# Hybrid attention and delta-rule layer on one core: solved blocks loaded ahead of the last head's copies, weight loads ordered behind casts, the last queries rotated on VectorE, the last results scaled on ScalarE

## The chip, the cores and the metric

The kernel runs on one core of one Trainium2 chip. The metric is device time in microseconds of one execution. The engines are TensorE (PE, with its weight loads as PEld), VectorE (DVE), ScalarE (ACT), GpSimd (POOL) and SyncE (SP). SP issues most DMAs, ACT issues the loads of the input weights; a queue issues its DMAs in the order in which they were placed on it.

## The reference

One layer for 1024 latent tokens and 256 context tokens of width 1024. Both are normalised and modulated (shift and scale from `c`), and go through one input projection of 4112 columns. Half of the mixing width is neighbourhood attention (8 heads of 64, a window of 8 x 16 in a 16 x 64 grid, plus all context keys in one softmax, with a learned bias). The other half is a gated delta rule in chunks, in both directions, with 4 heads of 128:

```python
a = jnp.where(pos[:, None] > pos[None, :],
              jnp.einsum('nbhid,nbhjd->nbhij', kb, k) * decay, 0.0)
t_inv = lax.linalg.triangular_solve(eye + a, ..., lower=True, unit_diagonal=True)
u = jnp.einsum('nbhij,nbhje->nbhie', t_inv, v * beta[..., None])
w = jnp.einsum('nbhij,nbhjd->nbhid', t_inv, kb * jnp.exp(gc)[..., None])
def step(state, xs):
    v_new = u_n - w_n @ state
    o_n = q_n @ state + qk_n @ v_new
    state = state * gl_n + k_n.T @ v_new
```

Its queries, keys and values go through a convolution over five tokens and SiLU; queries and keys are normalised, and those of the latent tokens are rotated by two axial angles. The scan's results are normalised. Both halves are multiplied by a SiLU gate each, concatenated, projected by `w_out`, normalised and added to the input.

## The kernel before, in words

Float32 products are made of three matmuls of split numbers: a weight is loaded raw, cast to its high part on ACT, and the low part is the difference, taken on POOL, or on DVE for every second quarter of the weights "nv0" (`load_w`, lines 550 to 573). The raw, high and low parts have 3, 4 and 4 buffers, which all input weights share.

The instructions are written in one order, and a planner that simulates the engines then puts the instructions of each engine in an order of its own: what is ready in its simulation goes by the order of writing, which `tc.high_priority(offset=n)` moves forward, and `order(r, before)` (line 169) keeps one instruction behind another without adding a wait. On the chip each engine works strictly in the order so planned.

The stages are these. `phase0` does the norms and the first projections. `phase2` (line 922) goes over the four heads of the delta rule. For each, it convolves Q, K and V (steps of one letter), turns Q and K to tokens and rotates them (T, `qk_tok`, line 1026), turns V (U), turns Q and K back (B), and, a head later, makes the chunk matrices (F, `delta_front`, line 1141). R is a part of the output gate. The letters p stand for one unit each of other projections (`projections`, line 981): three gates, then pair 1 of the attention, then the attention values in five units with the weights nv0, then pairs 2 and 3. 18 units come before the pairs 2 and 3, of which 14 stand in `phase2`'s strings of letters (lines 972) and 4 at the start of `phase_a2` (line 1644).

The inverse of each chunk's 128 x 128 matrix is made from 32 x 32 blocks. `delta_front` writes its matrices to `pm_dram`, and four DMAs copy their diagonal blocks to `ab_dram` (line 1175). There are 320 blocks in three groups. Two groups of 120 (heads 0 to 2) are solved together on DVE by `inv_pairs` (line 1195), in 30 levels of two operations, between the steps of head 3; the solved blocks are stored in `yd` (line 1216). The last 80 (head 3) are solved by `inv_blocks` (line 1218) in `phase_a2`. `inv_merge` (line 1241) then puts the blocks of a head together, in six parts named l, t, z, u, w, e in the string `MERGES` (line 138): l loads the matrices (pm, line 1247) and the solved blocks (vl, line 1258), t turns them with DVE's block transpose, z and u, w and e are small matmuls with copies between them, and e stores the result `tm`. One tm buffer serves the second direction of all four heads. `phase_a2` runs through the last 14 projection units with two generators beside them: `blocks` (the last group, then the masks and the loads of attention pair 0) and `merges`, at 4 and 1.5 steps per unit.

`phase_b` then interleaves the attention (`na_attn`, line 727) with the scan (`delta_scan`, line 1350), and `phase4` does the output projection. At the end of a pair's half, `values` in `na_attn` takes the reciprocal of twice the softmax sums (lines 762 and 763) and POOL spreads it over 512 elements (line 767); after a transposition on PE (line 773) it scales the result. `delta_end` (line 1457) scales a head's results by the norm's root; for the last head on DVE, in two halves (line 1471). `rsqrt` (line 196) adds and takes the power on POOL. "rho" is the root of the queries' norms of all heads; it is made in `delta_load` of head 0 (line 1345).

## Time and profile before

| | |
|---|---|
| median of 3 runs | 859.28 us (858.21 to 862.28) |
| profiled execution | 858.73 us, span 857.0 us |
| PE, PEld | 821.8 us (96%), 703.2 us (82%) |
| DVE, ACT, POOL | 498.9, 415.1, 359.1 us |
| granted PE clock, mean | 0.978 |

The profile is one execution, taken by the hardware profiler. Times in its rows count from the start of the span. A row of a window gives the stretch, its length, the busy time of PE, PEld, DVE, ACT and POOL with the number of instructions, the clock granted to PE as a share of full speed, the share of time in which the DMA engines were busy, and the GB/s they moved. A row of the order in time gives start, length, engine, line and operation, output and inputs, and in brackets the idle time before it with what ended it. A row of waits gives who waited for whom, the sum in us, the times, and the longest.

### The profile page before, as it was taken

The page shows a single profiled execution, that of the slowest core. Times are in us where ns is not written, and L with a number is a line of the kernel's source. Part 1 is how long each engine was busy: PE and PEld are TensorE (multiplying, and loading weights), DVE is VectorE, ACT ScalarE, POOL GpSimd, SP SyncE. Part 2 cuts the span into 40 slices and gives each one's busy share as a digit, 9 for nine tenths or more (in the row PEclk, how much of TensorE's full clock was granted, in tenths as well). Part 3 has the DMA queues.
Part 4 walks back from the last instruction along what each step waited for, and adds up shares of the span by engine and source line. Part 5 has one row for each costly group of instructions (what it writes and reads, how often), then busy time and mean ns, then how long its engine had stood idle before and what let it go on. Part 6 is the DMA issues. An engine that isn't in the chain of part 4 may idle for free.

```text
span 857.0 us, 16622 instructions
## 1 busy us (share of the span) xinstructions
PE 821.8 (96%) x6170; PEld 703.2 (82%) x6170; DVE 498.9 (58%) x998; ACT 415.1 (48%) x1089; POOL 359.1 (42%) x433
## 2 busy tenths in 40 slices
PE   8999999999999999979988999999999999999996
PEld 6788887888888778769876888888888988878885
DVE  4673454556376677699718953456556666653242
ACT  3372535654654753742215433566666666734121
POOL 0042221454482483562542202556747569525121
PEclk9999999999999999999997999799999999999998
DMA  8986442255526718723697599995958934134261
GB/s 333 337 293 214 142 129 89 86 173 185 144 86 212 225 51 275 196 80 116 212 237 234 177 256 273 412 247 192 279 154 271 238 114 160 39 111 135 98 197 50
DMA packets 86343, 159.67 MB, mean 186 GB/s; under 512 B 18405, under 2 KB 45750, under 8 KB 84086
## 3 DMA queue, kind: packets, MB, share of 16 engines
q1 hardware_dynamic: 78774, 144.94, 53.6%
q10 hardware_dynamic: 7488, 13.67, 5.5%
q8 instruction: 49, 0.80, 0.4%
q14 instruction: 32, 0.26, 0.1%
HBM read 109.51 MB, written 52.42 MB: 189 GB/s over the span
## 4 chain that ended last, share of the span: by engine, by line
PE 78%; DVE 8%; DMA 6%; ACT 3%; issue 3%; SPq 1%; POOL 1%; ACTq 0%; DVEq 0%; POOLq 0%
PE py L1525 3%; PE py L1527 3%; PE py L1526 3%; PE pz L587 3%; PE pz L588 3%; PE pz L583 3%; PE pa L1415 3%; PE pa L1426 2%; PE po L917 2%; PE tr L900 2%; PE po L912 2%; PE sc L882 2%; PE pv L598 2%; PE pv L597 2%; PE pv L596 2%
## 5 line engine op out<-in xcount | busy, mean ns | idle before, releaser
L887 ACT ACTIVATE pt<-pt,nm 128x544 f32<-128x544 f32 (+1 forms) x64 | 50.5, 790 | 39.2 <-DVE nm L886 38.8
L886 DVE CUSTOM_DVE_ANT_0 pt<-sc,gm 128x544 f32<-128x544 f32 (+1 forms) x64 | 49.4, 772 | 32.6 <-PE sc L882 27.0
L870 POOL TENSOR_TENSOR gm<-gt,mk 128x288 f32<-128x288 f32 (+1 forms) x48 | 46.5, 972 | 28.8 <-DVE nm L886 28.5
L1387 POOL TENSOR_SCALAR kd<-kt,kd 128x128 f32<-128x128 f32 x72 | 42.7, 605 | 25.2 <-PE pa L1426 20.7
L1015 DVE SCALAR_TENSOR_TENSOR acc_v<-xp_v,cols,acc_v 128x1282 f32<-128x1282 f32 x16 | 33.8, 2111 | 27.3 <-ACT acc_v L1013 26.9
L1168 POOL TENSOR_SCALAR_AFFINE_SELECT qe<-qe 128x256 f32<-128x256 f32 x32 | 28.9, 906 | 40.7 <-DVE qe L1167 40.7
L1591 DVE TENSOR_TENSOR finv<-py,ggb 128x512 f32<-128x512 f32 (+1 forms) x17 | 10.7, 657 | 50.7 <-ACT finv L1590 42.3
L583 PE MATMUL pz<-hh,wh_gz 128*128 128x512 f32 x96 | 39.1, 408 | 0.0
L587 PE MATMUL pz<-hl,wh_gz 128*128 128x512 f32 x96 | 39.1, 407 | 0.0
L588 PE MATMUL pz<-hh,wl_gz 128*128 128x512 f32 x96 | 39.0, 406 | 0.0
L1149 ACT ACTIVATE em<-em,gc 128x128 f32<-128x128 f32 x80 | 25.5, 390 | 25.2 <-DMA em<-gc_dram 23.9
L598 PE MATMUL pv<-wl_nv,hh 128*128 128x264 f32 x104 | 30.9, 300 | 4.8 <-DVE wl_nv L566 4.8
L1429 DVE SCALAR_TENSOR_TENSOR s<-s,egl,pa 128x128 f32<-128x128 f32 x64 | 19.7, 344 | 27.2 <-PE pa L1426 27.2
L1164 DVE SCALAR_TENSOR_TENSOR pm<-pk,nsc,em 128x128 f32<-128x128 f32 x80 | 23.5, 344 | 18.8 <-PE pk L1157 13.4
L1393 POOL TENSOR_SCALAR vb<-v,beta 128x128 f32<-128x128 f32 x40 | 24.1, 604 | 19.5 <-DVE y L1399 17.5
L900 PE MATMUL tr<-c,pt 128*96 128x128 f32 (+1 forms) x192 | 32.2, 277 | 0.0
L898 ACT COPY tcx<-tc 128x256 f32<-128x256 f32 x64 | 23.4, 366 | 16.1 <-PE tc L896 15.7
L566 POOL TENSOR_TENSOR wl_gz<-wr_gz,wh_gz 128x512 fp32r<-128x512 f32 x12 | 15.5, 1294 | 37.5 <-ACT wh_gz L565 35.9
L903 ACT COPY tl<-tr 96x384 f32<-96x384 f32 (+1 forms) x64 | 30.5, 476 | 0.0
L597 PE MATMUL pv<-wh_nv,hl 128*128 128x264 f32 x104 | 30.3, 294 | 0.0
L596 PE MATMUL pv<-wh_nv,hh 128*128 128x264 f32 x104 | 29.6, 296 | 0.0
L1415 PE MATMUL pa<-y,tm 128*128 128x128 f32 x144 | 25.3, 296 | 4.5 <-DVE y L1399 4.5
(470 smaller groups left out, 2853.1 us busy)
## 6 DMA issues: line engine op xcount, KB each, us to landing
wada<-in_w_ada SPq DMA_DIRECT2D x16, 512.0 KB
em<-gc_dram SPq DMA_DIRECT2D x20, 256.0 KB
pm_dram<-pm SPq DMA_DIRECT2D x20, 256.0 KB
tm_dram<-tm SPq DMA_DIRECT2D x8, 640.0 KB
kk<-qk_dram SPq DMA_DIRECT2D x16, 320.0 KB
tm<-tm_dram SPq DMA_DIRECT2D x4, 1280.0 KB
kq_dram<-kq SPq DMA_DIRECT2D x4, 1152.0 KB
kq<-kq_dram SPq DMA_DIRECT2D x4, 1152.0 KB
```

The lines of the kernel that those rows point to most:

```text
L583: r = nc.tensor.matmul(ps, wh, xh, start=(k == 0 and first), stop=False)
L587: nc.tensor.matmul(ps, wh, xl, start=False, stop=False)
L588: nc.tensor.matmul(ps, wl, xh, start=False, stop=(k == KC - 1))
L596: nc.tensor.matmul(ps, xh, wh, start=(k == 0), stop=False)
L597: nc.tensor.matmul(ps, xl, wh, start=False, stop=False)
L598: nc.tensor.matmul(ps, xh, wl, start=False, stop=(k == KC - 1))
L870: r = nc.gpsimd.tensor_tensor(self.gm[hh][:, 384 - n:384].rearrange("p (n c r) -> p n c r", c=nco, r=4), gv, self.mk[:, mo:mo + n].rearran ...
L886: nc.vector.tensor_tensor_reduce(pt[:, 384 - n:], sc[:, 512 - n:768], gm[:, 384 - n:], -1.0, 3.0e38, ALU.add, ALU.min, nm)
L887: self.last_exp = nc.scalar.activation(pt[:, 384 - n:], pt[:, 384 - n:], AF.Exp, bias=nm, scale=-1.0, accum_out=sums[:, ct, hh:hh + 1]).in ...
L900: self.pe(nc.tensor.transpose(pl[:m, rc * P:(rc + 1) * P], pt[:, 384 + (rc - 3) * m:384 + (rc - 2) * m], self.ident))
L1387: r = nc.gpsimd.tensor_scalar(kd[d], kt_[:, t, :], self.kd[:, h, d, t:t + 1], None, ALU.mult)
L1415: self.pe(nc.tensor.matmul(pa, tm[:, d, t, :], y[d], start=True, stop=True))
```

## The change

- **SP's queue.** The four copies of head 3's diagonal blocks leave `delta_front` and are issued in `blocks`, behind the loads of vl of the merge that has been issued by then. The loads of pm stand behind vl. The masks and pair 0's loads stand behind a vl, too.
- **ACT's queue.** A weight's load stands behind the cast before last.
- **DVE.** The additions of `inv_pairs` stand behind the last weight split written before them; a step has three levels in place of two. The rotation of the last head's queries moves from POOL to DVE.
- **POOL.** The root rho stands behind the last root taken before it. The spread of the reciprocals multiplies by 0.5, and the doubling on DVE is gone.
- **Order of writing.** The strings of `phase2` and `MERGES` change; nv0 is loaded one unit earlier; one more unit stands in `phase2` and one fewer at the start of `phase_a2`; the first step of `blocks` is moved forward by 800 in place of 300. With `while not self.vl_last: yield` that first step now returns without an instruction.
- **ACT** scales the last head's results, in eight operations.

```diff
-MERGES = "0l 0t 1l 0z 1t 0u 0w 2l 0e 1z 1u 2t 1w 1e 3l 2z 2u 3t 2w 2e 3z 3u 3w 3e"
+MERGES = "0l 0t 1l 0z 1t 0u 0w 0e 2l 1z 1u 2t 1w 3l 1e 2z 2u 2w 3t 2e 3z 3u 3w 3e"
...
-    def rsqrt(self, pool, x, n, tag, eps):
+    def rsqrt(self, pool, x, n, tag, eps, after=None):
         y = pool.tile([P, n], F32, name=f"rq_y_{tag}", tag=f"rq_y{n}")
-        self.nc.gpsimd.tensor_scalar(y, x, eps, None, ALU.add)
-        self.nc.gpsimd.tensor_tensor(y, y, bc(self.mhalf, [P, n]), ALU.pow)
+        r = self.nc.gpsimd.tensor_scalar(y, x, eps, None, ALU.add)
+        if after:
+            self.order(r, after)
+        self.last_root = self.nc.gpsimd.tensor_tensor(y, y, bc(self.mhalf, [P, n]), ALU.pow).ins.name
...
-            (load or nc.scalar.dma_start)(raw.rearrange("p k n -> p (k n)"), bass.AP(
+            r = (load or nc.scalar.dma_start)(raw.rearrange("p k n -> p (k n)"), bass.AP(
...
-                nc.scalar.copy(hi, raw)
-                (nc.vector if halves > 2 and k0 % 4 else nc.gpsimd).tensor_tensor(lo, raw, hi.bitcast(F32), ALU.subtract)
+                if r and len(self.casts) > 1:
+                    self.order(r, self.casts[-2])
+                self.casts.append(nc.scalar.copy(hi, raw).ins.name)
+                r = (nc.vector if halves > 2 and k0 % 4 else nc.gpsimd).tensor_tensor(lo, raw, hi.bitcast(F32), ALU.subtract)
+                self.split = r.ins.name
...
-            nc.vector.tensor_scalar(rs, sums[p, rt].rearrange("p a b -> p (a b)"), 2.0, None, ALU.mult)
-            nc.vector.reciprocal(rs, rs)
+            nc.vector.reciprocal(rs, sums[p, rt].rearrange("p a b -> p (a b)"))
...
-            nc.gpsimd.tensor_copy(rb[j], bc(rs.unsqueeze(2), [P, 8, 64]))
+            nc.gpsimd.tensor_scalar(rb[j], bc(rs.unsqueeze(2), [P, 8, 64]), 0.5, None, ALU.mult)
...
-                for c in ("RVpppTUpB", "RppVTpUBp", "RVTpUpB", "VRppTppUB")[h]:
+                for c in ("RpVppTUpB", "RppVpTpUB", "RVTpUpB", "VRppTpppUB")[h]:
...
-        yield from self.na_proj(pool, self.ps, [1])
-        w = self.load_w(self.wp, [(1024, 264)], 264, "nv0", halves=4)
+        for i, _ in enumerate(self.na_proj(pool, self.ps, [1])):
+            if i == 6:
+                w = self.load_w(self.wp, [(1024, 264)], 264, "nv0", halves=4)
+            yield
...
-                    eng = nc.gpsimd if which else nc.vector
+                    eng = nc.gpsimd if which and h < 3 else nc.vector
...
+        if h < 3:
+            self.inv_blocks_out(h)
+
+    def inv_blocks_out(self, h, after=None):
         ad, pd = self.ab_dram[:, :], self.pm_dram[h][:, :, :, :]
         for b in range(4):
-            nc.sync.dma_start(bass.AP(ad.tensor, ...
+            r = self.nc.sync.dma_start(
+                bass.AP(ad.tensor, ...
+            if after:
+                self.order(r, after)
...
-            nc.vector.tensor_tensor(ab[:, :, 0:m, m + 1:], ab[:, :, 0:m, m + 1:], t3, ALU.add)
-            if m % 2 == 0:
+            r = nc.vector.tensor_tensor(ab[:, :, 0:m, m + 1:], ab[:, :, 0:m, m + 1:], t3, ALU.add)
+            if self.split:
+                self.order(r, self.split)
+            if m % 3 == 0:
...
-            nc.sync.dma_start(pm[d][0:96], self.pm_dram[h][0:96, d])
...
-            nc.sync.dma_start(vl[32 * b:32 * b + 20], self.yd[g][10 * i:10 * i + 20].rearrange("t j i -> t (j i)"))
+            r = nc.sync.dma_start(vl[32 * b:32 * b + 20], self.yd[g][10 * i:10 * i + 20].rearrange("t j i -> t (j i)"))
+        self.vl_last = r.ins.name
+        for d in range(2):
+            self.order(nc.sync.dma_start(pm[d][0:96], self.pm_dram[h][0:96, d]), self.vl_last)
...
-            self.rho = self.rsqrt(self.cp, self.ssq.rearrange("p h t -> p (h t)"), 32, "rho", 4 * EPS)
+            self.rho = self.rsqrt(self.cp, self.ssq.rearrange("p h t -> p (h t)"), 32, "rho", 4 * EPS, self.last_root)
...
-                sl = slice(4 * gr, 4 * gr + 4)
-                nc.vector.tensor_tensor(o[:, sl], o[:, sl], bc(r[:, sl].unsqueeze(2), [P, 4, P]), ALU.mult)
+                for t in range(4 * gr, 4 * gr + 4):
+                    nc.scalar.activation(o[:, t, :], o[:, t, :], AF.Copy, scale=r[:, t:t + 1])
...
             def blocks():
+                while not self.vl_last:
+                    yield
+                self.inv_blocks_out(3, self.vl_last)
...
+                self.gate = self.vl_last
                 self.load(self.mk, self.I["masks"])
+                self.gate = None
...
+                self.gate = self.vl_last
                 self.na_pairs = {0: self.na_load(None, 0)}
+                self.gate = None
...
-            for _ in range(4):
+            for _ in range(3):
                 next(pr)
...
-                            with tc.high_priority(offset=300):
+                            with tc.high_priority(offset=800):
```

More of the change, by code (lines that the diff above doesn't have):

```diff
@@ L971, in phase2 @@
                     blocks = self.inv_pairs(cv)
-                for c in ("RVpppTUpB", "RppVTpUBp", "RVTpUpB", "VRppTppUB")[h]:
+                for c in ("RpVppTUpB", "RppVpTpUB", "RVTpUpB", "VRppTpppUB")[h]:
                     step(h, c)
-                    next(blocks, None)
+                    if h < 3 or c not in "":
+                        next(blocks, None)
             step(3, "F")
@@ L1172, in delta_front, with inv_load, inv_groups, inv_blocks_out @@
                 nc.sync.dma_start(self.qe_dram[h][:, :, t0 - 2:t0, :], qe)
+        if h < 3:
+            self.inv_blocks_out(h)
+    def inv_blocks_out(self, h, after=None):
         ad, pd = self.ab_dram[:, :], self.pm_dram[h][:, :, :, :]
         for b in range(4):
-            nc.sync.dma_start(bass.AP(ad.tensor, ad.offset + (80 * h + 20 * b) * 1024, [[32, 32], [1024, 20], [1, 32]]),
-                              bass.AP(pd.tensor, pd.offset + 32 * b * (20 * P + 1), [[20 * P, 32], [P, 20], [1, 32]]))
+            r = self.nc.sync.dma_start(
+                bass.AP(ad.tensor, ad.offset + (80 * h + 20 * b) * 1024, [[32, 32], [1024, 20], [1, 32]]),
+                bass.AP(pd.tensor, pd.offset + 32 * b * (20 * P + 1), [[20 * P, 32], [P, 20], [1, 32]]))
+            if after:
+                self.order(r, after)
+    def inv_load(self, g, ab):
+        nc = self.nc
+        n = min(120, 320 - 120 * g)
+        nc.sync.dma_start(ab[:n], self.ab_dram[120 * g:120 * g + n])
+        ab = ab[:n].rearrange("p (a b) -> p a b", a=32)
+        return ab
+    def inv_groups(self, gs, tile):
+        abs_ = [self.inv_load(g, tile(f"ab{g}", S)) for g in gs]
+        vbs = [tile(f"vb{g}", S) for g in gs]
+        tb = tile(f"tb{gs[0]}", 256 * len(gs))
+        yield
+        yield from self.inv_blocks(gs, abs_, vbs, [tb[:, 256 * i:256 * i + 256] for i in range(len(gs))])
+    def inv_blocks_out(self, h, after=None):
+        ad, pd = self.ab_dram[:, :], self.pm_dram[h][:, :, :, :]
+        for b in range(4):
+            r = self.nc.sync.dma_start(
+                bass.AP(ad.tensor, ad.offset + (80 * h + 20 * b) * 1024, [[32, 32], [1024, 20], [1, 32]]),
+                bass.AP(pd.tensor, pd.offset + 32 * b * (20 * P + 1), [[20 * P, 32], [P, 20], [1, 32]]))
+            if after:
+                self.order(r, after)
     def inv_load(self, g, ab):
@@ L1604, in phase_a2 @@
         with tc.tile_pool(name="a2", bufs=1, side="right", reuse_waits="tile") as ap:
-            ready = self.ready
+            ready, self.vl_last = self.ready, None
             buf = lambda nm, tag, n: self.pf.tile([P, n], F32, name=f"{nm}_{tag}", tag=tag)
             def blocks():
+                while not self.vl_last:
+                    yield
+                self.inv_blocks_out(3, self.vl_last)
                 vv = buf("ab", "vv", 2 * S)
@@ L1675, in run @@
             self.setup(ctx)
+            self.casts, self.split = [], None
             dt = lambda nm, shape: self.dp.tile(shape, F32, name=nm)
```

## The prediction

> **What bounds the kernel now.** I read the page first, then the waits of TensorE (PE), then the rows of the clock, then the chain of waits and the order in time around each stretch where PE stands still.
>
> ```profile
> span 857.0 us, 16622 instructions
> PE 821.8 (96%) x6170; PEld 703.2 (82%) x6170; DVE 498.9 (58%) x998; ACT 415.1 (48%) x1089; POOL 359.1 (42%) x433
> ...
> PE tz L1280 <- DVE ld L1268: 5.7, 1, 5.7
> PE pv L598 <- DVE wl_nv L566: 4.8, 1, 4.8
> ```
>
> PE is busy for 96% of the span, so a microsecond of the other engines is worth something only where PE waits for them, or where PE runs slowly. Two single waits make 10.5 us. The windows give what follows each (columns: stretch; length; PE, PEld, DVE, ACT and POOL busy; granted clock; DMA share; GB/s).
>
> ```profile
> 382.70:388.70 6.00, 6.00 (x28) 6.00 (x29) 5.73 (x11) 4.20 (x18) 6.00 (x4) 0.52 0.36 115
> 453.20:460.20 7.00, 6.99 (x91) 5.88 (x92) 5.32 (x8) 5.28 (x13) 3.06 (x5) 0.51 0.86 285
> 527.60:543.00 15.40, 13.54 (x221) 12.29 (x221) 7.03 (x16) 4.70 (x11) 8.41 (x16) 0.64 0.87 333
> 760.00:770.00 10.00, 8.19 (x53) 5.77 (x52) 6.89 (x9) 1.76 (x6) 5.04 (x5) 1.00 0.62 234
> ```
>
> After each long wait PE works at half the clock: 6.0 x 0.48 = 2.9 us and 7.0 x 0.49 = 3.4 us more. So the first hole (weights of nv0) costs 4.8 + 2.9 = 7.7 us, the second (solved blocks) 5.7 + 3.4 = 9.1 us. The third stretch, where the last merges have no projection beside them, costs 1.9 us idle and 15.4 x 0.36 = 5.5 us of clock. The last head's end costs 1.8 us idle, at full clock.
>
> **The first hole.** PE waits for a split of nv0 (line 566) that VectorE (DVE) does late:
>
> ```profile
> 378.64 2.98 POOL L1061 TENSOR_TENSOR tok<-tok,rot 128x512 f32<-128x512 f32 x2
> 379.05 1.45 DVE L1208 TENSOR_TENSOR tb<-ab 120x336 f32<-120x336 f32 x1
> 380.53 1.45 DVE L1210 TENSOR_TENSOR ab<-ab,tb 120x336 f32<-120x336 f32 x1
> 381.91 0.74 DVE L566 TENSOR_TENSOR wl_nv<-wr_nv,wh_nv 128x528 fp32r<-128x528 f32 x1
> 389.30 0.65 DVE L1208 TENSOR_TENSOR tb<-ab 120x468 f32<-120x468 f32 x1
> 381.58 5.71 POOL L199 TENSOR_TENSOR rq_y_rho<-rq_y_rho,mhalf 128x32 f32<-128x32 f32 x1
> 387.27 0.25 POOL L198 TENSOR_SCALAR rq_y_g<-ss 128x10 f32<-128x10 f32 x1
> ...
> L1059 DVE TENSOR_TENSOR rot<-tok,rope x8: 681/685/689, 181.8 to 396.0; 128x512 f32<-128x512 f32 x8
> ```
>
> While POOL rotates the last head's queries, a block step of 336 elements takes DVE 1.45 us; later, with POOL in its power function, one of 468 takes 0.65. The change takes these six POOL operations (6 x 1.49, half of 2.98, is 8.9 us) and gives DVE six of 0.69 = 4.1 us; four block operations of the rows shown or like them fall by about 0.9 each, so DVE comes out about even here. What helps PE is the order: nv0 (four loads, casts and splits) is issued one step earlier, and the later block additions stand behind its last split. A block operation already ahead of it, and the rotation's 4.1 us, can still delay it. I take 6.5 of the 7.7 us as gained; bounds 0 (the rotation and the block levels issued before it, now three to a step in place of two, stand ahead of it instead) and 7.7. The rho root (0.52 + 5.71 us on POOL) moves behind the key root: keys come up to 5.7 us earlier, and rho is next wanted only by the scan's ends, far later.
>
> **The second hole.** SyncE's queue and then the chain of waits show it:
>
> ```profile
> 429.07 2.60 SPq L1175 DMA_DIRECT2D ab_dram<-pm_dram  x4
> 431.76 1.03 SPq L1216 DMA_DIRECT2D yd<-ab  x2
> 436.59 1.17 SPq L1184 DMA_DIRECT2D ab_vv<-ab_dram  x1
> 437.81 1.21 SPq L1247 DMA_DIRECT2D pmf<-pm_dram  x2
> 439.41 2.05 SPq L1258 DMA_DIRECT2D vl<-yd  x4
> ...
> 440.84 8.78 DMA vl<-yd
> 453.21 2.34 PE tz L1280 x80
> ```
>
> The solved blocks (yd) are stored only after four copies of the last head's blocks have been issued, and loaded (vl) only after the last group's load and two loads of pm; they land 8.8 us after that, among the copies' small packets. The change moves those copies (four DMAs, 2.6 us of issue) and the group load behind vl, and the two pm loads too; the masks and pair 0's loads are held behind a vl as well. So yd can go at least 431.76 - 429.07 = 2.7 us earlier in the queue and vl another 2.4 (the rows of 436.59 and 437.81), and it lands without the copies beside it: the last head's vl, which has none, is waited for 4.99 us (row of 506.07 below), 3.8 less than 8.8. That is 8.9 us, before the earlier keys, against 5.7 needed. What is late next is pm, which the same matmuls read. I take 7.5 of 9.1 us; bounds 0 and 9.1.
>
> The clock is where a rule bears on this. The Trainium skill, TensorE: Matmul & The Clock Gate, Part 1, says that a gate halves PE's clock after about 3.4 us without work and gives it back after about as long a busy stretch. The rows above agree with the halving after 4.8 and 5.7 us, though the slow stretches last 6 to 7 us. By that rule a wait that is only cut below 3.4 us loses its whole slow stretch, too; by the rows alone, in proportion, half a wait would leave half of 2.9 and 3.4 us. It would raise case C below by 1.7 us of gain and leave the forecast.
>
> **What is late next: the last head's own merge.** Its blocks are inverted last, on DVE, and no projection covers the end:
>
> ```profile
> 496.26 0.19 DVE L1233 TENSOR_TENSOR ab_vv<-ab_vv,tb_qh 80x31 f32<-80x31 f32 x1
> 506.07 1.25 DVE L1266 STREAM_TRANSPOSE vx<-vl 128x1024 f32<-128x1024 f32 x1 [4.99 <-DMA vl<-yd]
> 529.85 1.96 POOL L1289 COPY tm<-ld 32x320 f32<-32x320 f32 x4 [18.04 <-DMA tm_dram<-tm]
> 527.53 0.24 PE pz L588
> 536.97 0.72 PE sc L879 x2
> 430.00:440.00 10.00, 10.00 (x55) 8.59 (x54) 0.69 (x1) 1.50 (x3) 8.03 (x9) 1.00 0.94 285
> 462.00:497.00 35.00, 35.00 (x552) 28.38 (x551) 32.31 (x73) 14.74 (x31) 7.10 (x8) 1.00 0.57 180
> ```
>
> From 442 (its load issued at 436.59) to 496.4 the group's solve shares a DVE that is busy 32.3 of 35 us. The copies now start after vl, so its load stays near 437 even if vl moves up by some 8 us; and the first call of its generator, which carries the raised priority (800), now only returns, since vl is not yet issued. PE arrives 14 us earlier (6.5 + 7.5). The chain gains about 6 us from merge work that DVE does earlier (it was busy 0.69 of the 10 us from 430), 3 of the 9.8 us between 496.3 and 506.1, as pair 0's loads now stand behind vl, and about 2 from the new merge order, which has head 2's "w" before head 3's "t" and so stores the shared tm sooner. 14 - 11 = 3 us come back: +3. Bounds: -7.4 (third stretch gone) and +9 (the chain gains only 5).
>
> **The rest.**
>
> ```profile
> 310.00:320.00 10.00, 8.44 (x46) 6.67 (x46) 4.80 (x6) 4.40 (x15) 8.85 (x10) 1.00 0.09 27
> 763.17 3.44 DVE L1471 TENSOR_TENSOR o<-o,rq_y_o 128x512 f32<-128x512 f32 x2 [2.40 <-POOL rq_y_o L1464]
> 767.36 0.63 PE L773 MATMUL prt<-c,rb 128*128 128x128 f32 x4 [1.63 <-DVE zs L760]
> L1418 ACT ACTIVATE vn<-pa,beta x40: 347/366/381, 543.2 to 756.3; 128x128 f32<-128x128 f32 x40
> L762 DVE TENSOR_SCALAR rs<-sums x8: 160/182/2067, 561.5 to 753.0; 128x8 f32<-128x8 f32 x8
> L767 POOL COPY rb<-rs x8: 599/612/618, 565.5 to 753.6; 128x512 f32<-128x512 f32 x8
> 593.17 0.60 POOL L767 COPY rb<-rs 128x512 f32<-128x512 f32 x1
> 598.09 0.60 PE L773 MATMUL prt<-c,rb 128*128 128x128 f32 x4
> L1387 POOL TENSOR_SCALAR kd<-kt,kd x72: 592/603/629, 540.0 to 745.8; 128x128 f32<-128x128 f32 x72
> ```
>
> Scaling on ScalarE: eight operations by 0.37 = 2.9 us in place of 3.44 on DVE, on an engine busy 1.76 of 10 us there. DVE's product of line 760 no longer stands behind them, and PE's wait of 1.63 goes: -1.7; bounds 0 and -1.8. The eight doublings of line 762 go: 8 x 0.18 and one of 2.07, at most -2. In their place the POOL copy of 0.61 us becomes a multiplication over 512 elements: from 0.61 (the copy) to 4 x 0.605 = 2.4 (line 1387 scaled up), that is 0 to +1.8 each, 0 to 14.5 us of POOL in all, for a result that PE wants some 4 us after it is there in the pair of rows shown (593.8 against 598.1). Where that cover is gone the whole could come to PE. I take 0 for the pair, bounds -2 and +6. The GPSIMD Engine Reference of the Trainium skill, section 4.1, calls one-input work there about line rate, which would make it 0.6; no row here shows a multiplication of this size, and by it the sum stays as it is.
>
> Before 370 us, where steps move one place: PE idles there once, 1.6 us in the row from 310. Loads on ScalarE's queue now stand behind the cast before last: their issue (0.33 us) adds no semaphore, it only keeps two weight halves in flight in place of three, while PE needs 24 matmuls of 0.23 us, 5.5 us, for two. I take 0; bounds -1.6 and +3 (one missed half).
>
> Sum against the profiled execution's 858.73 us (span 857.0 and 1.7 around it): -6.5 - 7.5 + 3 - 1.7 = -12.7, 846.0. The median shown, 859.28, lies 0.55 higher: 846.5.
>
> **Rivals.** A is the forecast.
> B, nothing comes back at the end: both holes whole, the third stretch half gone: -7.7 - 9.1 - 3.7 - 1.8 = -22.3, 837. For it: DVE's idle time from 430; against: the shared tm.
> C, only the first hole goes, and PE waits for pm or for vl's buffers in place of vl: -6.5 - 1.7 + 1 = -7.2, 852. For it: pm now follows vl, and vl's memory is cleared at line 1254 only when the front's last tiles are free.
> D, it does not do what it says: DVE, busy 19.45 of 20 us from 370 to 390, gets the rotation ahead of the split, the wait only changes its name, and the end takes back the rest: 0 - 7.5 + 9 - 1.7 = -0.2, 859.
>
> ```profile
> 370.00:390.00 20.00, 14.32 (x88) 13.43 (x87) 19.45 (x24) 10.66 (x46) 19.23 (x12) 0.83 0.23 71
> ```
>
> E, slower: the last head's copies start too late. If vl is issued no earlier than now, they go at 441.5 in place of 429.07, 12.4 us later; the solve, head 3's merge and the first scores follow by as much, and all that PE saved is waited for there: 858.73 + 12.4 - 1.7 - 3 = 866.4, 867 in the median's terms. It decides from about 9 us of delay of the copies on; against it stand the earlier yd and the 9.8 us of slack between 496.3 and 506.1.
>
> **How the numbers follow.** Chances: A 0.50 (own range 841 to 852), B 0.13, C 0.14, D 0.12, E 0.11. Half a per cent, 4.3 us, is about what a measurement of this kernel tells from no change. Faster: A, B and most of C, 0.75; within: D and a little of C, 0.14; slower: E, 0.11. The range leaves out E and about half of B: 836 to 861.
>
> **What would show it.** Right: no wait of line 598 for line 566 near 380 and a clock row of 1.00 there; vl issued before pm and before the copies, landing in under 5 us; no wait over 2 us of line 1280; on PE, line 773 without its 1.63. The last stretch before the scores should be longer than 9.4 us (527.5 to 537.0). Wrong: a clock row near 0.5 between 370 and 470, the last group's solve ending after 500, or line 773 waiting for line 767.

## The result, and the profile after

The changed kernel takes 863.76 us (median of 16 runs, 859.85 to 866.35), the kernel before 858.37 us beside it (16 runs, 853.34 to 862.87). The ratio is 1.0059, with a 95% interval of 1.0039 to 1.0080: slower by 0.6%, where 846.5 us was forecast. Its profiled execution takes 865.87 us, with a span of 864.2 us against 857.0.

Executions of one kernel differ by some ten microseconds, and a profile shows only one of them. So the stages below are compared as distances inside one profile, and the verdicts rest on the ratios.

First the stages on PE (windows; columns as in the prediction), for the kernel before and for the changed one:

```profile
370.00:400.00 30.00, 24.32 (x170) 23.43 (x169) 29.31 (x40) 12.57 (x51) 19.68 (x12) 0.89 0.27 83
400.00:440.00 40.00, 40.00 (x245) 35.86 (x244) 24.45 (x60) 9.10 (x18) 18.98 (x22) 1.00 0.66 212
440.00:470.00 30.00, 24.31 (x294) 19.49 (x293) 20.40 (x39) 12.09 (x25) 7.11 (x8) 0.83 0.88 240
...
527.00:560.00 33.00, 30.78 (x368) 27.41 (x368) 15.24 (x40) 15.11 (x41) 18.80 (x30) 0.79 0.93 360
```

```profile
370.00:400.00 30.00, 27.76 (x216) 26.66 (x215) 25.29 (x49) 15.82 (x56) 14.45 (x6) 1.00 0.34 106
400.00:440.00 40.00, 37.45 (x211) 32.35 (x211) 30.69 (x65) 8.51 (x17) 20.03 (x22) 1.00 0.63 201
440.00:470.00 30.00, 24.79 (x302) 19.96 (x301) 15.84 (x24) 12.97 (x27) 6.79 (x9) 0.89 0.89 222
...
527.00:560.00 33.00, 20.04 (x199) 18.42 (x200) 7.68 (x19) 8.04 (x21) 12.66 (x21) 0.59 1.04 373
```

The first hole is nearly gone: 27.76 of 30 us at full clock, where PE had 24.32 at 0.89. But 2.5 us are missing from 400 to 440, where none were, the second hole has hardly shrunk, and from 527 to 560 PE is busy for 20 us at a clock of 0.59, where it had 30.8 at 0.79. The waits of PE in the changed kernel, from 370 to 560, name what stands there:

```profile
PE tz L1357 <- POOL tm L1333: 10.9, 1, 10.9
PE tu L1343 <- issue: 3.2, 1, 3.2
PE tu L1343 <- ACT zt L1328: 3.2, 2, 3.0
PE pk L588 <- DVE sl_q L664: 2.1, 1, 2.1
PE tz L1324 <- DVE ld L1312: 2.0, 1, 2.0
PE pv L603 <- POOL wl_nv L570: 1.5, 1, 1.5
```

(Lines of the changed kernel are some 40 higher behind 1200: L1324 is L1280 of the kernel before, L1333 is L1289, L1357 is L1313, L1370 is L1326.) Line 588 waits for an operation that DVE does right behind the end of the pairs' solve. The wait of 10.9 us is head 3's "w", which needs POOL's copy into the shared tm, which needs the stores of head 2's tm. In order of time, SP, DVE, POOL and PE of the changed kernel:

```profile
431.63 0.22 DVE L1250 TENSOR_TENSOR ab<-ab,tb 120x60 f32<-120x60 f32 x1
...
431.88 0.79 SPq L1258 DMA_DIRECT2D yd<-ab  x2
437.35 1.41 SPq L1299 DMA_DIRECT2D vl<-yd  x4
...
447.66 3.61 SPq L1299 DMA_DIRECT2D vl<-yd  x4
453.93 3.58 SPq L1212 DMA_DIRECT2D ab_dram<-pm_dram  x4
...
461.37 0.39 SPq L1224 DMA_DIRECT2D ab_vv<-ab_dram  x1
...
503.02 0.19 DVE L1275 TENSOR_TENSOR ab_vv<-ab_vv,tb_qh 80x31 f32<-80x31 f32 x1
...
522.80 0.39 PE L593 MATMUL pz<-hh,wl_gz 128*128 128x512 f32 x1
...
531.56 0.33 SPq L1370 DMA_DIRECT2D tm_dram<-tm  x1
534.74 1.05 SPq L1370 DMA_DIRECT2D tm_dram<-tm  x1
...
542.23 1.96 POOL L1333 COPY tm<-ld 32x320 f32<-32x320 f32 x4 [33.48 <-DMA tm_dram<-tm]
...
548.29 0.58 PE L883 MATMUL sc<-kk,qh 128*128 128x256 f32 x1
...
808.26 0.60 ACT L1634 ACTIVATE finv<-py 128x512 f32<-128x512 f32 x1 [9.50 <-PE py L1571]
```

and the answering rows of the kernel before:

```profile
426.03 0.22 DVE L1210 TENSOR_TENSOR ab<-ab,tb 120x60 f32<-120x60 f32 x1
...
527.36 0.39 PE L588 MATMUL pz<-hh,wl_gz 128*128 128x512 f32 x1
...
536.90 0.58 PE L879 MATMUL sc<-kk,qh 128*128 128x256 f32 x1
...
801.13 0.60 ACT L1590 ACTIVATE finv<-py 128x512 f32<-128x512 f32 x1 [9.80 <-PE py L1527]
```

In this profile the pairs' solve ends 5.6 us later; not all of that is the kernel's (see "The first hole" below). The last head's copies leave at 453.93 and not at 429.07: behind head 2's load of solved blocks, not head 0's. The last group's solve ends 6.8 us later (503.02 against 496.26). From there to the first scores it is 45.3 us where it was 40.6 (536.90 less 496.26): 4.6 more. From the first scores to the first row of the last output it is 260.0 where it was 264.2: 4.2 less. 6.8 + 4.6 - 4.2 is the 7.2 us of the span. That PE ends the projections 4.6 us earlier (522.80 against 527.36) is in none of these terms: it is waited out. These are the terms of two profiles, not of the kernels.

### The profile page after: what moved, and what is told of

Its sections match the earlier page's. It is cut to its first block, busy times and chain, and to the rows that moved or that the text cites. A ratio compares the mean times of both kernels' runs of the same rounds, so it can differ in the third digit from the quotient of the medians.

```text
span 864.2 us, 16623 instructions
## 1 busy us (share of the span) xinstructions
PE 819.9 (95%) x6170; PEld 699.3 (81%) x6170; DVE 490.8 (57%) x994; ACT 419.5 (49%) x1097; POOL 359.4 (42%) x427
## 4 chain that ended last, share of the span: by engine, by line
PE 69%; DVE 11%; DMA 10%; ACT 3%; POOL 3%; issue 2%; SPq 1%; ACTq 0%; DVEq 0%; POOLq 0%
PE py L1569 4%; PE py L1571 3%; PE py L1570 3%; PE pz L588 3%; PE pz L593 3%; PE pz L592 3%; PE pa L1459 3%; DMA kk<-qk_dram 2%; PE po L921 2%; PE pa L1470 2%; PE tr L904 2%; PE po L916 2%; PE sc L886 2%; DMA pm_dram<-pm 2%; PE gpl_k L588 2%
## 5 line engine op out<-in xcount | busy, mean ns | idle before, releaser
L1022 DVE SCALAR_TENSOR_TENSOR acc_v<-xp_v,cols,acc_v 128x1282 f32<-128x1282 f32 x16 | 30.7, 1919 | 30.4 <-ACT acc_v L1020 17.8
L1333 POOL COPY tm<-ld 32x320 f32<-32x320 f32 x16 | 7.2, 452 | 61.1 <-DMA tm_dram<-tm 54.4
```

The lines of the kernel that those rows point to most:

```text
L1022: nc.vector.scalar_tensor_tensor(av, xp[:, s0 + tap:s0 + tap + 1282 - s0], wc(tap), av, ALU.mult, ALU.add)
```

## The experiments

The theories are C (the copies leave late and all behind them follows), S (the store's place in SP's queue), G (the gate on pair 0's loads), D (the DMA engines), T (what PE wins before the scores is waited out there), and those of the single parts. Every kernel is held against the kernel before on the same chip, and the changed kernel's ratio to it is 1.0059. e1 to e4 ran on one chip, e5 to e8 on a second, e9 to e15 on a third. The distances in the text are read from these rows of each profile (the starts of the first copy, of the solve's last operation and of the first scores):

| run | ratio (95%) | copies of head 3 | last solve ends | first scores | distance |
|---|---|---|---|---|---|
| before | 1 | 429.07 | 496.26 | 536.90 | 40.6 |
| changed | 1.0059 (1.0039 to 1.0080) | 453.93 | 503.02 | 548.29 | 45.3 |
| e1 | 1.0054 (1.0030 to 1.0078) | 446.94 | 496.38 | 540.77 | 44.4 |
| e2 | 1.0035 (1.0012 to 1.0058) | 436.03 | 495.28 | 545.26 | 50.0 |
| e3 | 1.0006 (0.9986 to 1.0026) | 418.90 | 495.47 | 543.17 | 47.7 |
| e4 | 1.0062 (1.0039 to 1.0084) | 449.94 | 503.55 | 543.35 | 39.8 |
| e5 | 1.0011 (0.9983 to 1.0039) | 419.22 | 496.09 | 543.21 | 47.1 |
| e6 | 0.9949 (0.9923 to 0.9975) | 418.41 | 497.13 | 538.58 | 41.5 |
| e7 | 0.9928 (0.9896 to 0.9960) | 427.78 | 494.78 | 535.45 | 40.7 |
| e8 | 1.0014 (0.9983 to 1.0045) | 425.00 | 494.78 | 536.13 | 41.4 |
| e9 | 0.9962 (0.9935 to 0.9990) | 415.20 | 490.19 | 530.77 | 40.6 |
| e10 | 0.9970 (0.9942 to 0.9999) | 429.52 | 497.42 | 538.10 | 40.7 |
| e11 | 0.9974 (0.9948 to 1.0000) | 426.94 | 493.72 | 531.51 | 37.8 |
| e12 | 0.9978 (0.9949 to 1.0008) | 431.06 | 498.25 | 539.06 | 40.8 |
| e13 | 1.0015 (0.9992 to 1.0038) | 436.08 | 494.72 | 536.70 | 42.0 |
| e14 | 0.9981 (0.9962 to 1.0001) | 418.92 | 497.67 | 538.51 | 40.8 |
| e15 | 0.9976 (0.9957 to 0.9995) | 410.11 | 496.59 | 536.99 | 40.4 |

### e1: the store on another queue

```diff
-            nc.sync.dma_start(self.tm_dram[h][:, d], tm[d])
+            (nc.scalar if h == 2 else nc.sync).dma_start(self.tm_dram[h][:, d], tm[d])
```

> Edit: the two stores of head 2's merged matrices (tm_dram<-tm, L1370) are issued on ScalarE's queue instead of SP's, so that they no longer stand behind the loads of the first attention pair; nothing else. Theory S (the store's place in the queue is the loss): in the changed kernel PE waits 10.9 us in one piece at L1357 for the POOL copy L1333, which waits for these stores, issued at 531.56 and 534.74 though head 2's last result stood at about 524.4; on another queue they go out at about 525, the wait falls to under 4 us, and the time falls by 6 to 9 us to 855 to 858. Theory C (the last head's copies leave too late, and all behind them is late): the scores still wait for the first pair's loads, whose last issue is at 533, so the wait only changes its name; 861 to 864. Theory D (the DMA engines are the bound from 512 to 560, with a share of 1.04 to 1.08): the stores land late wherever they are issued; 862 to 865.

No gain that can be measured: 860.84 us against 856.94. The stores leave at 525.23 and 527.49 in place of 531.56 and 534.74, but in this execution all before 500 was some 6 us earlier. Head 2's last result stands at 517.81 here and at 524.45 in the changed kernel, so the later store leaves 9.7 us behind it where it was 10.3. On ScalarE's queue the stores waited, too: around the first one ScalarE does nothing for 10.2 us, until a load has landed. POOL's copy then comes at 534.71, 7.2 us behind the later store, and the DMA engines are busy throughout:

```profile
525.66 0.93 ACT L1332 COPY xo<-vd 32x320 f32<-32x320 f32 x2 [10.17 <-DMA ql<-qk_dram]
...
520.00:530.00 10.00, 4.73 (x79) 4.29 (x79) 0.93 (x2) 2.25 (x5) 0.00 (x0) 0.56 1.09 276
530.00:540.00 10.00, 4.29 (x45) 4.15 (x45) 2.60 (x6) 0.84 (x2) 4.98 (x10) 0.50 1.03 418
```

The distance from the last solve to the scores fell by 0.9 only. So the edit hardly brought the store forward and decides neither S nor D: of the 17 us from the result to POOL's copy, some ten lie ahead of the store's issue and seven behind it. Behind the scores, PE waited 3.9 us for a load of qe that it does not wait for in the changed kernel.

### e2: the raised priority on a step that does something

```diff
-                        elif first:
+                        elif first and self.vl_last:
```

> Edit: the raised priority of 800 goes to the first step of the blocks that does something (the last head's copies) and not to the empty step before the first load of solved blocks exists. By the order of issue this puts the copies right behind head 0's load of solved blocks and ahead of head 1's and head 2's, where the changed kernel has them behind head 2's (453.93). Theory C (late copies are the loss): copies at about 439 to 442 instead of 453.93, the last group's solve ends 9 to 12 us earlier (491 to 494 instead of 503.0), head 3's merge no longer ends last, and the time falls by 7 to 11 us to 853 to 857. Theory S: head 2's stores still stand behind the first pair's loads, but these start earlier as the gate opens earlier; 857 to 861. Theory D: 860 to 864.

861.49 us against 856.94, 2 us better than the changed kernel by the ratios, which is within their intervals. The copies leave at 436.03 and the last solve ends at 495.28, in time; but the scores come 50.0 us behind it. So C is right up to the solve, and not the whole: something else holds the scores.

### e3, e5 and e6: copies back, then the order of merges, then the gate

e3 puts the four copies back into `delta_front`. e5 also restores the old string `MERGES`. e6 also takes the gate from pair 0's loads:

```diff
-        if h < 3:
-            self.inv_blocks_out(h)
+        self.inv_blocks_out(h)
...
-                while not self.vl_last:
-                    yield
-                self.inv_blocks_out(3, self.vl_last)
...
-                self.gate = self.vl_last
                 self.na_pairs = {0: self.na_load(None, 0)}
-                self.gate = None
```

> Edit: the one part named first in the change is undone, the last head's copies go back to where the kernel before has them (ahead of the solved blocks), all other parts stay. Theory C: the solve of the last group ends at 496 or before as in the kernel before, the scores start near 530 to 534, and the part was worth +8 to +11 us: 853 to 856. Theory S: the head-2 stores still wait behind the gated loads; 858 to 862. The prediction's own sum, by which this part opens the second hole of 9.1 us again: 866 to 871.

> Edit: as in the run with the last head's copies back, and the order of the merge steps as in the kernel before too. With the copies back alone the time was 1.0006 of the kernel before, and its scores still started at 543.17 and not at 536.90, since head 1's last step came at 505.4 (501.28 before), head 2's u and w steps behind it, and head 3's POOL copy at 537.11 (529.85). Theory M (the new order of the merge steps is the rest of the loss): scores at 535 to 538, ratio 0.992 to 0.995. Theory G (the gate on the first pair's loads is the rest): no change against the copies back alone, 0.999 to 1.002.

> Edit: copies and order of merge steps back, and the first pair's loads no longer ordered behind the last load of solved blocks. What stays of the change is the first hole's part (earlier weight load, waits of weight loads, order of the solve behind the splits), the solved blocks ahead of the masks and of each head's own matrices, the turn of the last queries on VectorE, the order of steps before 370, and the end. Theory G: scores at 533 to 537, ratio 0.990 to 0.994. Theory M: the same as with copies and order back. Theory T (the stretch before the scores is set by the last group's solve and by the DMA engines, and what TensorE wins ahead of it is only waited out there): scores at 536 to 539 whatever is undone, so that only the 4.2 us won behind the start of the scores are left: 0.995 to 0.997.

856.79 against 856.94; 858.31 against 858.10; 853.15 against 858.10 us. The copies' place costs 0.0053 (4.5 us), the order of the merge steps nothing that can be measured (a gain of 2 us would lie within the intervals), the gate 0.0062 (5.3 us). M falls. The gate shows in the way of one store. In order of time, SP and POOL in e5, with the gate:

```profile
526.02 1.25 SPq L1369 DMA_DIRECT2D tm_dram<-tm  x2
...
537.15 1.96 POOL L1332 COPY tm<-ld 32x320 f32<-32x320 f32 x4 [23.79 <-DMA tm_dram<-tm]
```

and in e6, without it:

```profile
525.74 1.40 SPq L1369 DMA_DIRECT2D tm_dram<-tm  x2
...
532.60 1.96 POOL L1332 COPY tm<-ld 32x320 f32<-32x320 f32 x4 [21.91 <-DMA tm_dram<-tm]
```

Head 2's stores are issued at the same time, yet POOL gets the buffer 4.6 us later with the gate, and the scores start 4.6 us later. Counted from head 2's last result the difference is larger: it stands at 522.46 in e5, so that the store also waits 3.6 us for its issue, and at 526.74 in e6, where the second store waits for nothing else. In e3, which has the gate, the first store leaves at 524.55, less than 1 us behind its result, and POOL's copy still comes 12.6 us behind it. The gated loads come later and closer together: the DMA engines' share is 1.08 and 1.02 in the two windows from 520 to 540 in e5, 1.00 and 0.86 in e6. That the store lands late because it stands among them is argued from this; no run takes their bytes away. The table says the same over all runs: with the gate the distance from the last solve to the scores is 44.4 to 50.0 us (changed, e1, e2, e3, e5), without it 37.8 to 42.0.

### e4: the gate alone taken away

The same edit as e6's last part, on the changed kernel.

> Edit: the loads of the first attention pair are no longer ordered behind the last load of solved blocks (gate taken from them alone; the masks keep it). By the order of issue three of their loads move ahead of head 3's load of solved blocks, the others stay behind it since they wait for buffers. Theory G (the gate is the loss): the loads start near 503 instead of 512.06, the stores of head 2 are freed 5 to 9 us earlier, 856 to 859. Theory C: most of the loads wait for buffers that the late solve and merge hold, so the gate costs 0 to 2 us: 862 to 865.

862.67 us against 856.94: no gain, though the distance fell to 39.8 and the scores came 4.9 us earlier in the profile. That profile then has PE waiting 2.5 us for qe, as in e1. POOL's copy comes 11.4 us behind the store, as with the gate (11.1 in e5) and not as in e6 (6.9): so the gate is not the only thing that makes the store land late. Why the gate costs nothing beside late copies and 5 us without them is not settled; G and C are not simply added.

### e7, e10 and e11: the end alone

The kernel before with both end parts (e7), with ScalarE's alone (e10), with the reciprocal's alone (e11). These parts are the only edits, as in the change itself:

```diff
-                nc.vector.tensor_tensor(o[:, sl], o[:, sl], bc(r[:, sl].unsqueeze(2), [P, 4, P]), ALU.mult)
+                    nc.scalar.activation(o[:, t, :], o[:, t, :], AF.Copy, scale=r[:, t:t + 1])
...
-            nc.vector.tensor_scalar(rs, ..., 2.0, None, ALU.mult)
-            nc.vector.reciprocal(rs, rs)
+            nc.vector.reciprocal(rs, ...)
-            nc.gpsimd.tensor_copy(rb[j], bc(rs.unsqueeze(2), [P, 8, 64]))
+            nc.gpsimd.tensor_scalar(rb[j], bc(rs.unsqueeze(2), [P, 8, 64]), 0.5, None, ALU.mult)
```

> Edit: the kernel before with two parts of the change alone, ScalarE scaling the last head's results and the factor 2 moved from VectorE's tensor_scalar into the POOL operation (tensor_scalar in place of a copy). From the start of the scores to the first row of the last output the kernel before takes 264.2 us and the changed one 260.0. If these two parts are the whole of it, 852.5 to 854.5 and ratio 0.994 to 0.997; by the prediction's own term (1.7 us at the end, 0 for the POOL operation) ratio 0.997 to 0.9985; if the 4.2 us come from elsewhere (the later start itself, with more loads already landed), 1.000.

> Edit: the kernel before with one part alone, ScalarE scales the last head's results in eight operations where VectorE did it in two. The two end parts together gave ratio 0.9928 (0.9896 to 0.996). The prediction's term for this part is 1.7 us: ratio 0.998. If it is the larger share of the two, 0.994 to 0.996; the waits in question are those of line 773 (1.63 us, once) and of the last y rows.

> Edit: the kernel before with the other part alone, the factor 2 is taken from VectorE's eight doublings into the POOL operation, which becomes tensor_scalar by 0.5 in place of a copy. The prediction took 0 with bounds of -2 and +6: ratio 0.998 to 1.007. If a POOL tensor_scalar of 128x512 takes 2.4 us (four times the 0.605 of 128x128) it shows in the groups of the profile, and the time is 1.000 to 1.003; if it takes 0.6 as the copy does, the eight doublings are won, one of them 2.07 us long ahead of the end: 0.996 to 0.998.

852.92 us against 858.10 with both: the lowest ratio of all kernels measured, though e6's interval overlaps with it. 855.18 and 854.71 against 857.75 singly: 2.6 and 2.2 us by the ratios, about equal shares, though either interval reaches to 1 or nearly so. In e10 the wait of line 773 is gone; in e11 it stands (1.6 us), and the longest wait of PE for y falls from 1.7 to 0.5 us. POOL's multiplication of 512 elements, of which no row of before had the size, reads in e7's groups:

```profile
L766 POOL TENSOR_SCALAR rb<-rs 128x512 f32<-128x512 f32 x8 | 11.9, 1494 | 7.0 <-DVE rs L762 7.0
```

### e8, e9, e14 and e15: what closes the first hole

e8 is the kernel before with the earlier weights, the ordered weight loads and the solve behind the splits. e9 is e6 without these. e15 is e7 with the rotation of the last queries on VectorE, e14 with the steps' order and the rho root, too. The first lines below are what e8 puts in and e9 takes out, the last pair the rotation:

```diff
-        w = self.load_w(self.wp, [(1024, 264)], 264, "nv0", halves=4)
+            if i == 6:
+                w = self.load_w(self.wp, [(1024, 264)], 264, "nv0", halves=4)
+            if self.split:
+                self.order(r, self.split)
...
-                    eng = nc.gpsimd if which else nc.vector
+                    eng = nc.gpsimd if which and h < 3 else nc.vector
```

> Edit: the kernel before with the first hole's part alone (the weights of nv0 loaded from the seventh step of the projections on, weight loads ordered behind casts, the pairs' solve ordered behind the splits). The prediction's sum: the hole at 370 to 380 with its half clock is 7.7 us of which 6.5 are won in time: 850 to 852, ratio 0.991 to 0.994. Theory T: TensorE is done with the projections 5 to 6 us earlier, but the scores wait for the last group's solve and the loads behind it, and start at 535 to 538 as before: ratio 0.998 to 1.002.

> Edit: as in the run with copies, merge order and gate back (ratio 0.9949), and the first hole's part undone too: the weights of nv0 are loaded after the projections' second block of steps, weight loads don't stand behind casts, the pairs' solve doesn't stand behind the splits and is cut two levels to a step. In that run the hole is closed (PE 10.0 of 10 us in 380 to 390, clock 1.00), yet the pairs' solve ends at 430.81 and not at 426.25, PE waits 2.1 us for line 664 near 428, and the scores start at 538.58, later than in the kernel before. Theory H (the hole is not closed but handed on: VectorE's solve ends as much later as the splits go ahead, and the second hole and line 664's wait take it back): with the part undone the time is the same or less, ratio 0.990 to 0.997. The prediction's sum (6.5 us of gain): ratio 1.001 to 1.004.

> Edit: the kernel before with the two end parts, the last queries turned on VectorE, the rho root behind the key root, and the steps of the front in the changed order; weight loads, casts, the solve's order and pace, and everything behind 430 stay as in the kernel before. The run without the first hole's part had that hole closed all the same (PE 9.75 and 10.0 of 10 us from 370 to 390) and its pairs' solve ended at 427.3, 1.3 later than in the kernel before and 4.5 earlier than in the changed one. Theory R (the rotation and the steps close the hole, and the earlier weights with the solve behind the splits only make the solve late): ratio 0.985 to 0.990, the hole's 6 us on top of the ends' 0.9928. Theory T (what PE wins before 400 is waited out before the scores): 0.992 to 0.996.

> Edit: the kernel before with the two end parts and the last queries turned on VectorE, steps in their old order. If the rotation alone closes the first hole (POOL no longer works beside VectorE's block steps, which took 1.45 us for 336 elements there): PE over 9 of 10 us in 370 to 380 and in 380 to 390, the wait for line 566 under 2 us, and the time as with the steps reordered too. If VectorE's six operations of 0.69 stand ahead of the split instead: the wait stays at 4 to 5 us, ratio 0.993 to 0.998.

859.11 against 858.10, 854.78 against 857.75, 855.43 and 854.97 against 857.37 us. e8 didn't do what it was made for; its waits still have

```profile
PE pv L601 <- DVE wl_nv L568: 4.7, 1, 4.7
```

so the part that was meant for the hole doesn't close it, and its ratio tells nothing about a closed hole. The rotation alone does. In e15's waits and in DVE's order of time:

```profile
PE pv L598 <- DVE wl_nv L566: 0.5, 1, 0.5
...
375.31 1.28 DVE L1060 TENSOR_TENSOR tok<-tok,rot 128x512 f32<-128x512 f32 x2
376.86 0.69 DVE L566 TENSOR_TENSOR wl_nv<-wr_nv,wh_nv 128x528 fp32r<-128x528 f32 x1
379.07 0.51 DVE L1207 TENSOR_TENSOR tb<-ab 120x336 f32<-120x336 f32 x1
```

e9, where the hole's own part is gone and the rotation stays, has PE busy for 9.75 and 10.0 of 10 us from 370 to 390, and its ratio of 0.9962 is that of e6, 0.9949, within the intervals: H stands, in that the part wins nothing. The windows of e7, and then of e15, which differs from it by the rotation only:

```profile
370.00:400.00 30.00, 24.31 (x175) 23.12 (x174) 29.17 (x43) 13.98 (x52) 19.67 (x12) 0.94 0.27 83
400.00:440.00 40.00, 40.00 (x245) 35.85 (x245) 26.33 (x64) 9.50 (x19) 18.97 (x22) 1.00 0.70 219
440.00:470.00 30.00, 26.00 (x308) 20.81 (x307) 20.27 (x39) 13.14 (x28) 7.15 (x8) 0.89 0.85 232
470.00:500.00 30.00, 30.00 (x494) 24.81 (x493) 25.46 (x60) 12.34 (x28) 4.33 (x6) 1.00 0.58 181
```

```profile
370.00:400.00 30.00, 29.45 (x227) 28.24 (x226) 28.75 (x55) 13.97 (x52) 11.20 (x7) 1.00 0.46 154
400.00:440.00 40.00, 39.03 (x217) 33.74 (x216) 27.44 (x53) 7.72 (x15) 21.20 (x23) 1.00 0.71 204
440.00:470.00 30.00, 24.36 (x297) 19.26 (x296) 22.44 (x40) 13.36 (x28) 5.65 (x7) 0.89 0.65 183
470.00:500.00 30.00, 28.23 (x442) 23.26 (x440) 22.95 (x56) 10.95 (x24) 4.42 (x6) 0.89 0.55 177
```

PE wins 5.1 us of busy time and 1.8 us of clock before 400. Then it gives back 1.0 us, 1.6 us, and 1.8 us with 3.3 us of clock (30 x 0.11) up to 500; the last matmul of the projections starts at 526.15 against 525.93 and the first scores start at 536.99 against 535.45. The pairs' solve ends at 426.62 against 426.22 (57.8 and 54.8 us behind the start of V's last convolution), so what follows it comes no earlier, and PE merely meets it sooner. The time, 0.9976 against 0.9928, is no better; by the ratios it is even 0.5% worse, though both profiles have a span of 852.0 us, and that is not explained. This is T, for the first hole, with a ratio just above the range that T was given; R falls.

### e12: pm behind vl, beside the ends

```diff
-            nc.sync.dma_start(pm[d][0:96], self.pm_dram[h][0:96, d])
...
+        for d in range(2):
+            self.order(nc.sync.dma_start(pm[d][0:96], self.pm_dram[h][0:96, d]), self.vl_last)
```

> Edit: the kernel before with the two end parts, and each head's own matrices (pm) loaded behind its solved blocks (vl); copies, masks, gate, merge order and the first hole stay as in the kernel before. This is what is left of the move when it costs no copy its place. By the order of issue the first vl then stands ahead of both pm loads, 1.2 us of issue and 960 KB earlier. Theory V (the second hole shrinks by what vl gains): the wait of L1279 for ld falls from 4.0 to 5.7 us to under 3, ratio 0.988 to 0.991. Theory T (the scores wait for the last group's solve and for loads, not for PE): ratio 0.992 to 0.994, the same as with the ends alone. Theory P (the matmuls read pm too, which now comes last): a wait for pm of 2 to 4 us in its place, 0.993 to 0.997.

856.42 against 857.75 us. The wait for ld is 2.3 us here, 4.0 in e7 and 5.7 before; PE waits for zt instead (2.8 us, which e7 does not have), the copies of what those matmuls made. The time is no better than e7's; the ratios (0.9978 and 0.9928, from two chips) make this part cost 0.5%, with intervals that overlap. V falls.

### e13: the move without its two costs

e2's and e4's edits together.

> Edit: the changed kernel with the raised priority on the first step that does something (copies behind head 0's solved blocks and ahead of head 1's) and without the gate on the first pair's loads: the move as it is named, with neither of the two costs seen so far. Theory C+G (the two are the whole loss of the move: copies that leave 25 us late, and loads held behind the last solved blocks): the last group's solve ends at 494 to 497, scores at 536 to 540, ratio 0.993 to 0.997, as with the copies left in place. Theory V (the move then also wins its second hole): ratio 0.986 to 0.990. If another part of the move costs: over 0.999.

858.60 against 857.37 us: 0.0044 better than the changed kernel, and no better than the kernel before, though the end's 0.0072 are in it. In its profile, which is its fastest execution, the solve ends at 494.72 and the scores start at 536.70, as in the kernel before. So the two costs are much of the loss, but not all: e6, which differs by the place of the copies and the order of merges only, has 0.9949. With the copies between vl and pm, PE waits for pm, as in e2 (3.0 us) and in no other kernel:

```profile
PE tz L1324 <- DMA pmf<-pm_dram: 3.3, 2, 2.3
```

If this wait went into the time in full, which no run shows, it would be about half of the 0.0066 (5.7 us) between the two; the rest isn't explained. V falls: the move wins nothing even so.

## Why the prediction was wrong

**The forecast's sign.** Rival E came out, with a chance of 0.11: the last head's copies start too late. The sign that goes with it, the last solve ending after 500, came: 503.02. Its 866.4 us for the profiled execution is close to the 865.87, its 867 for the median is 3 us above the 863.76. That closeness is luck, as the sum was another: E had copies 12.4 us late and everything late by as much. They were 24.9 us late, and the solve only 6.8 (with the copies back, e3, it ends at 495.47). The other 4.6 us, of distance, go with the gate in e4 (39.8), which E didn't have; e4's time, though, is no better.

**The step that failed is "what is late next".** It lets the chain gain 11 us (6 by merge work done earlier, 3 because pair 0's loads stand behind vl, 2 by the new merge order), so that only 3 of 14 us come back. The chain lost 11.4 us: the first scores are at 548.29 against 536.90. The gate, entered as a gain of 3, cost 5.3 us once the copies were back (e5 against e6). The new merge order, entered at 2, gave nothing that can be measured (e3 against e5). The sentence that the copies "start after vl, so its load stays near 437" took the first place the order allows, behind head 0's vl, for the place they get; they stand behind head 2's, and the load came at 461.37. The prediction saw that the raised priority goes to a step that only returns, and left it without a price; e2 shows that it decides where the copies stand. Taken off one after the other, the parts of the change come to -6.2 us for the end (e7), +1.8 for all the rest of e6, +5.3 for the gate (e5), -0.4 for the merge order (e3) and +4.5 for the copies' place; each difference is uncertain by about 3 us, and in another order they could come out otherwise (e4). In place of -14 for the two holes and +3 behind them stand +1.8 and the cost of the gate and the copies.

**The first hole.** It closed nearly as forecast (27.76 us at clock 1.00), for another reason than the one given: the rotation closes it (e15), the earlier weights don't (e8). Rival D's reason did happen, as the rotation's six operations stand ahead of DVE's split in e15 (3.9 us, the last pair at 375.31) and in the changed kernel, but its consequence did not. The prediction's "about even" had four block operations fall by 0.9 each. Eight fell, those of 216 to 336 elements, from 10.0 us in e7 to 4.7 in e15, and those of 300 and 336 elements now stand behind the split. The -6.5 us was right at 400 and wrong as a term of the time. The two holes were added as if independent; but in e15, where the pairs' solve ends as before, a PE that comes 6 us sooner waits as much longer behind it.

In the changed kernel's profile that solve ends 5.6 us later, at 431.63. Of this, 1.6 us stand ahead of it already (V's last convolution starts at 371.44 against 369.88). The rest is not the kernel's alone: counted from that convolution the solve takes 60.1 to 60.2 us in the changed kernel, e3, e5 and e6, and 56.5 to 56.7 in e1, e2, e4 and e13, whose instructions on DVE and POOL are the same there; the kernel before has 56.2. The two groups differ by one split on POOL, that of the changed kernel and that of e1:

```profile
375.10 4.99 POOL L570 TENSOR_TENSOR wl_nv<-wr_nv,wh_nv 128x528 fp32r<-128x528 f32 x1 [9.31 <-ACT wh_nv L569]
...
373.38 1.35 POOL L570 TENSOR_TENSOR wl_nv<-wr_nv,wh_nv 128x528 fp32r<-128x528 f32 x1 [7.79 <-ACT wh_nv L569]
```

**The second hole.** -7.5 us forecast; from 440 to 470 PE gained 0.5 us of busy time and 1.8 us of clock. vl is issued at 437.35, 2.1 us earlier than in the kernel before and not 5, since yd itself comes no earlier in this profile (431.88 against 431.76), where the solve ends late. The forecast's 3.8 us of faster landing compared DVE's idle time before one load (4.99) with the way of another from its issue (8.8); still, DVE reads the first vl at 443.22 in place of 449.70, and PE's wait for it falls from 5.7 to 2.0 us. What is late next is not pm but the solved blocks of head 1: head 0's zt on ACT stands behind a copy that needs them, and PE waits 3.0 us for zt. In the chain of the changed kernel (start, length):

```profile
441.06 9.91 DMA vl<-yd
...
455.70 0.42 ACT zt L1328
```

In e1 and e4 the waits for ld and zt come to 2.1 and 2.3 us together, where the changed kernel has 5.2, and their profiled executions take 864.54 and 864.71 us against its 865.87. As far as these profiles tell, a smaller second hole is for the most part waited out, too.

**The end.** ScalarE's scaling was entered at -1.7 and the pair of POOL and DVE at 0. Together they gave 6.2 us (e7), singly 2.6 (e10) and 2.2 (e11). The pair of both was mis-sized: 1.7 lies outside e7's interval (3.4 to 8.9 us). Singly, -1.7 lies within e10's interval, and e11 came out at about its lower bound of -2.

**The multiplication on POOL.** 1.49 us in place of 0.61, inside the bounds of 0.6 and 2.4, and hidden, as taken. The Trainium skill, GPSIMD Engine Reference, section 4.1, calls one-input work there about line rate; the measurement differs from that here, as the multiplication of 512 elements takes 2.4 times the time of the copy of them.

The signs that the prediction named came out on both sides: no long wait at the first hole, vl ahead of pm and of the copies, no wait of line 773, and a last stretch before the scores of 25.5 us (522.80 to 548.29) in place of 9.4; against it, the last solve ending after 500 and a clock row near 0.5 between 370 and 470 (0.50 from 456.8 on, shown below).

## What to carry to other kernels

Two waits of one engine are separate gains only where different chains end them; ask of each wait what ends it, and whether that comes sooner too. An order that keeps traffic back to let one small load pass sends that traffic later, where a store on the critical chain can meet it. Before a difference between two profiles is put down to an edit, look for it in other runs with the same instructions. Where a generator's first step carries a priority, see that this step still holds an instruction.

## What the runs showed of the hardware that was not expected

A wait of 3.0 us was enough for half the clock. In the changed kernel PE's last matmul before it ends at 453.13; the clock falls between 456.4 and 456.8, just behind the wait's end, and stays at 0.50 up to 463:

```profile
456.17 0.21 PE L1343 MATMUL tu<-vd,zt 32*32 32x32 f32 x1 [3.04 <-ACT zt L1328]
...
456.40:456.80 0.40, 0.21 (x13) 0.20 (x14) 0.00 (x0) 0.38 (x2) 0.00 (x0) 0.72 0.87 151
456.80:457.20 0.40, 0.40 (x33) 0.40 (x30) 0.00 (x0) 0.38 (x2) 0.00 (x0) 0.50 0.42 88
```

The Trainium skill, TensorE: Matmul & The Clock Gate, Part 1, has a window of about 3.4 us without work for this. From the last matmul to the fall are about 3.4 us here, too, with a few small matmuls at their end. In the second hole of the kernel before they are less: the last matmul ends at 447.52, and the clock row is 0.94 from 449 to 450 and 0.50 from 450 on, about 2.4 us behind it. The rule that a wait cut below the window loses its whole slow stretch holds for the first hole, where 1.5 us are left and the clock row is 1.00; in the second, 3.0 us of wait still brought a slow stretch (456.6 to 463.4) about as long as that after 5.7 us (453.2 to 460.1).

An operation of POOL and those of DVE beside it can hold each other up, and which one gives way differs between executions. POOL's split of nv0 and a pair of DVE's rotation start within 0.1 us of each other in the changed kernel, e1 to e6 and e13. In e1, e2, e4 and e13 the split takes 1.3 us and the pair 2.4; in the others the split takes 5.0 us, to 1.2 us behind the end of DVE's own split, and the pair 1.3. The pairs' solve then ends some 3.6 us later.

A store issued at the same time set its buffer free 4.6 us later where the loads ahead of it had been held back and came together (e5 and e6).
